# Eight operand splits issued later and in program order, one small vector operation moved in the last product, and 64-byte gaps between the weight tiles of a two-layer decoder trunk

## The chip, the cores and the metric

The kernel runs on one core of a Trainium2 chip. The metric is the time of one execution on the device in microseconds (us). Three runs of the kernel before took 1043.71, 1044.87 and 1045.28 us; their median is 1044.87 us.

A core has a matrix engine (PE; its weight loads are listed apart as PEld), a vector engine (DVE), an activation engine (ACT), a general engine (POOL) and a queue engine (SP) that issues most transfers. Each of them works through its own list of instructions in order and waits at the head of its list for what the next instruction needs.

## What is computed

The reference is two layers on 1024 tokens of width 1024. The first is a gated layer over chunks of 128 tokens, the second is attention with a window of 128 tokens, 16 query heads and 4 key and value heads, one sink per head and a linear bias. Each layer ends in a product with an output matrix, a root-mean-square norm and a residual sum. What the change touches lies in the second layer:

```python
q, z = jnp.split(h @ w_in, 2, axis=-1)
...
logits = jnp.einsum('btkgd,bskd->bkgts', qb, kb).astype(jnp.float32) + alibi
...
p = jnp.exp(logits - m[..., None])
denom = jnp.sum(p, axis=-1) + jnp.exp(sink - m)
o = jnp.einsum('bkgts,bskd->btkgd', p.astype(vb.dtype), vb).astype(jnp.float32)
...
y = out * jax.nn.silu(z)
return y @ w_out
```

## The kernel before, in words

Operands are float32. Each operand of a large product is kept as a high part and a low part: `split` (L104 to L106) lets ACT copy the source to `hi` (L105) and DVE write `lo`, the source less `hi` (L106). `mm3` (L215 to L218) makes a product from three matmuls: hi by hi, hi by lo, lo by hi. Such a matmul is 128x128 by 128x512. The large products are done in the seven-product scheme for 2x2 blocks, so that some operands are sums of blocks.

The phases in order are the first layer (`v_layer`, `uz_layer`, `out_layer`), the products for queries, keys and values, and then `attn`. `attn` goes through 16 units, each one block of 128 tokens and one half of the heads. Beside the work of the units it hands out 120 pieces of other work, the fill: 80 steps of query and gate products, and then 40 steps `p0` to `p39` of the output product (`Out.early`). A step of the output product is six matmuls. The list `BY` (L1283) says up to which fill step each unit goes, and the string `ORDER` (L1281) says in which order a pass takes its parts: scores of both head groups, fill, exponentials, values of the unit two passes back, fill, exponentials, gate, normalise, transposes of the unit one pass back, post, fill, fill, normalise. Unit 15, the last, is worked on while steps `p19` to `p25` are handed out; its scores come ahead of `p19`, and the values of unit 13 right behind `p19`. The steps `p0` to `p15` write PSUM tiles `oc`, `p16` to `p23` write `od`, `p24` to `p39` write `oe`.

The products behind `p24` and behind `p32` need a sum of blocks as their operand, four token blocks t = 0 to 3 each; these are called sum m = 1 and sum m = 7. `Out.sums` (L1352) makes each of them in three moves at three steps that the table `SUMS` (L1284) gives as (m, t, load, add, split): at the first number `y_again` loads a block from DRAM into a tile of the tag `raw` (which has three buffers), at the second POOL adds the gated block to it (for m = 1 the sum goes into another tile), at the third `split` makes the operand's `hi` and `lo`. The move for step k is written behind the product's step k. The steps `p24` to `p27` read sum m = 1 for t = 0 to 3, and `p32` to `p35` read sum m = 7 for t = 0 to 3.

The order in the lists of the engines is the work of a scheduler, which may take an instruction early when its model says that the inputs are there. `held` (L1287) ties the attention parts on DVE and ACT to one another in the order written; fill instructions are free, unless `tc.keep_in_program_order` ties one behind the instruction that was written before it on the same engine.

`Out.late` is the end: the product `of`, 96 matmuls, first the half that `after3` closes and then, for each t, 12 matmuls, an add of the PSUM tile (`c`), its square sum on ACT, a product with the gain (`o`), and the norm's factor `r`, which POOL raises to the power -0.5. `final` (L1306) makes output rows, two DVE operations at L1309, for the t before. One DVE operation at L1447 turns the square sums of the first half into `ef` for all four t.

Tiles in the on-chip memory lie in pools one behind another: `big` (operands T, n, q, o), `const`, `wpool` (three `raw`, two `whi`, two `wlo` tiles of 4096 bytes per partition, in this order), `st`, and then pools that take turns. In the built program every tile of `big`, `wpool` and `st`, and all further ones that are matmul weights or the large moving operands, starts at 128 modulo 256 bytes. The identity used by the transposes (`ident`) starts at 96 modulo 256, and the tiles `pr` at 32.

Of the kernel before, what the change touches and what calls it, by code (L numbers as in the profile page):

```python
# [7 lines left out]
F32 = mybir.dt.float32  # L8
F32R = mybir.dt.float32r
BF16 = mybir.dt.bfloat16  # L10
U32 = mybir.dt.uint32
AF = mybir.ActivationFunctionType
ALU = mybir.AluOpType

P = 128
D = 1024
# [8 lines left out]
EPS = 1e-6  # L25
# [25 lines left out]
def tile_yoco(  # L51
# [19 lines left out]
    nc = tc.nc  # L71
# [4 lines left out]
    wpool = ctx.enter_context(tc.tile_pool(name="wpool", bufs=2))  # L76
# [4 lines left out]
    def bank(tag, name):  # L81
        return psum.tile([P, 512], F32, tag=tag, name=name)
# [8 lines left out]
    small = const.tile([P, 5], F32, name="small")  # L91
    nhalf = small[:, 0:4]
    nc.vector.memset(nhalf, -0.5)

    def raw_tile(name):
        return wpool.tile([P, 1024], F32, tag="raw", name=f"raw_{name}", bufs=3)
# [7 lines left out]
    def split(hi, lo, src):  # L104
        nc.scalar.activation(hi, src, AF.Copy)  # L105
        nc.vector.tensor_tensor(lo, src, hi.bitcast(F32), ALU.subtract)  # L106
# [19 lines left out]
    class Weights:  # L126
# [30 lines left out]
        def load(self, i):  # L157
            for n in range(min(len(self.raw), 20), min(i, 19) + 1):
                src, kind = self.order[n]
                if n < 20:  # L160
                    self.raw[n] = wload(src, f"w{n}")
# [48 lines left out]
    def wnext():  # L210
        w = weights.get()
        weights.ahead()
        return w

    def mm3(out, a_hi, a_lo, b_hi, b_lo, start, stop):  # L215
        nc.tensor.matmul(out, lhsT=a_hi, rhs=b_hi, start=start, stop=False, skip_group_check=True)  # L216
        nc.tensor.matmul(out, lhsT=a_hi, rhs=b_lo, start=False, stop=False, skip_group_check=True)  # L217
        nc.tensor.matmul(out, lhsT=a_lo, rhs=b_hi, start=False, stop=stop, skip_group_check=True)  # L218
# [33 lines left out]
    def add(out, a, b, op, eng=None):  # L252
        (eng or nc.vector).tensor_tensor(out, a, b, op)  # L253
# [297 lines left out]
    def uz_layer():  # L551
# [153 lines left out]
        for q in range(len(quads) + 1):  # L705
# [24 lines left out]
            if q > 0:  # L730
                product(q - 1, 3, pcc, False)
                add(pc[0, 1], pc[0, 1], pcc, ALU.add)
                scale(pc[0, 1], 1)
                if pz:
                    finish(pg, 0, 1)
                    sums(pg)
                    del grp[pg]
                else:
                    for i in range(2):
                        for j in range(2):  # L740
                            nc.scalar.activation(pc[i, j], pc[i, j], AF.Gelu_apprx_tanh)
                del ops[q - 1]
# [331 lines left out]
    def by_head(t):  # L1074

        return t.rearrange("p k t -> p (k t)").rearrange("p (m b g t) -> p m b g t", m=4, g=2, t=P)
# [204 lines left out]
    ORDER = "01FavFbgmtpFFn"  # L1281
    lags = {}
    BY = [6, 12, 19, 25, 32, 38, 45, 51, 57, 64, 71, 78, 85, 92, 99, 106, 112, 120]  # L1283
    SUMS = [(1, 0, 0, 2, 17), (1, 1, 3, 5, 18), (1, 2, 6, 8, 19), (7, 0, 8, 11, 18), (1, 3, 10, 12, 20), (7, 1, 14, 16, 21), (7, 2, 19, 21, 24), (7, 3, 23, 25, 28)]  # L1284
    behind = {}

    def held(what, *args):  # L1287
# [18 lines left out]
    def final(h, t, yo, r, xt, later=None):  # L1306
        for i in range(2):
            cs = slice(i * 512, i * 512 + 512)
            nc.vector.scalar_tensor_tensor(yo[i], yo[i], r, xt[:, cs], ALU.mult, ALU.add)  # L1309
            dst = out[h * TH + t * P:h * TH + (t + 1) * P, cs]  # L1310
            if later is not None:
                later.append((dst, yo[i]))
            else:
                (nc.scalar if (h, t, i) == (1, 3, 1) else nc.sync).dma_start(out=dst, in_=yo[i])
# [4 lines left out]
    def y_again(p, t):  # L1319
        r = raw_tile(f"y{p}_{t}_{len(again)}")  # L1320
        again[len(again)] = r
        load(r[:, 0:512], yd[p][t])
        return r[:, 0:512]

    class Out:
# [26 lines left out]
        def sums(self, plan):  # L1352
            todo = {}
            for m, t, *at in plan:
                for what in range(3):
                    todo.setdefault(at[what], []).append((what, m, t))
            raw = {}
            for at in range(max(todo) + 1):
                for what, m, t in todo.get(at, ()):
                    if what == 0:  # L1360
                        raw[m, t] = y_again(m == 1, t)
                    elif what == 1:
                        d = self.s1[t] if m == 1 else raw[m, t]
                        mix = [a.rearrange("p (a t) -> p a t", t=P) for a in (d, raw[m, t])]
                        add(mix[0], mix[1], self.z[0][:, :, t * P:(t + 1) * P], ALU.add, nc.gpsimd)
                        raw[m, t] = d
                    else:
                        if m not in self.o:
                            self.o[m] = big.tile([P, 2, 4, 4, P], F32R, tag={1: "P0a", 7: "P0b"}[m], name=f"o{m}")
                        split(*(self.o[m][:, e, t].rearrange("p m t -> p (m t)") for e in range(2)), raw[m, t])  # L1370
                yield

        def early(self):
# [31 lines left out]
            def products():  # L1405
                ps = [bank("mm", f"oc{t}") for t in range(4)]
                yield from self.product(ps, self.of(self.q0, 0), True, True, lambda t, p: copy(m4[t], p))
                yield from self.product(ps, self.of(self.q0, 1), False, True, after2)
                ps = [bank("mm", f"od{t}") for t in range(4)]
                yield from self.product(ps, self.of(self.q1, 0), True, True, after5)  # L1410
                ps = [bank("mm", f"oe{t}") for t in range(4)]
                yield from self.product(ps, sum_operand(1), True, True,
                                        lambda t, p: add(n2[t], n2[t], p, ALU.add))
                yield from self.product(ps, sum_operand(7), False, True, after7)

            sums = self.sums(SUMS)
            for _ in products():
                step(sums)
                yield

        def late(self):
            gp, n2, m5, q1 = self.gp, self.n2, self.m5, self.q1
            ps = [bank("s", f"of{t}") for t in range(4)]

            def after3(t, p):
                c = m5[t]
                add(c, c, p, ALU.add)
                self.square(1, 0, t, c)
                add(c, c, gp[0], ALU.mult, nc.gpsimd)

            for k, _ in enumerate(self.product(ps, self.of(q1, 1), True, False, after3)):
                if k < 4:
                    d = self.z[1][:, :, k * P:(k + 1) * P]
                    hi, lo = (by_head(w)[:, 0:2, k] for w in q1)
                    split(hi, lo, d.rearrange("p (m g) t -> p m g t", m=2))
                elif k == 4:
                    w = [wnext() for _ in range(2)]
                    for dst, src in self.stores:
                        tc.keep_in_program_order(nc.sync.dma_start(out=dst, in_=src))
                elif k == 5:  # L1440
                    final(*self.rest.pop(0))
                elif k == 6:
                    hf = big.tile([P, 4, D], F32, tag="P0a", name="hf1")
                    xt = [load(hf[:, t], h1d[1][t]) for t in range(4)]
            final(*self.rest.pop(0))
            ef = const.tile([P, 8], F32, tag="rpa", name="ef1")
            nc.vector.tensor_scalar(ef[:, 0:4], self.ss[1][:, 0], 1.0 / D, EPS, ALU.mult, ALU.add)  # L1447
            y = self.of(q1, 0)
            for t in range(4):
                for m in range(4):  # L1450
                    hi, lo = w[m // 2]
                    cs = slice(m % 2 * 512, m % 2 * 512 + 512)
                    a = y(t, m)
                    mm3(ps[t], a[0], a[1], hi[:, cs], lo[:, cs], False, m == 3)
                c, o, r = n2[t], self.m4[t], ef[:, 4 + t:5 + t]
                add(c, c, ps[t], ALU.add)
                self.square(1, 1, t, c)
                add(o, c, gp[1], ALU.mult)
                if t:
                    final(*self.rest.pop(0))  # L1460
                nc.vector.tensor_scalar(r, self.ss[1][:, 1, t:t + 1], 1.0 / D, ef[:, t:t + 1], ALU.mult, ALU.add)
                nc.gpsimd.tensor_tensor(r, r, nhalf[:, 0:1], ALU.pow)
                self.rest.append((1, t, [m5[t], o], r, xt[t]))
            final(*self.rest.pop(0))
# [85 lines left out]
```

## Time and profile before

| | |
|---|---|
| median of three runs | 1044.87 us |
| the profiled execution's own time | 1044.52 us |
| its span in the profile | 1042.8 us |
| mean granted PE clock | 0.993 |
| first matmul of step `p0` starts | 930.53 us |
| last matmul starts | 1033.10 us |

The profile is of one execution. Busy time is the time an engine spends in instructions; matmuls overlap, so that the start of the next one says more than the length of one. A row of the timeline has the start in us, the length in us, engine, line of the kernel, operation, the tile written and the tiles read, shapes, and the number of instructions merged into the row; in brackets stands how long the engine was idle just before it and what released it. A row of the windows view has, for each engine, the busy time and the number of instructions in a stretch of time, and then the granted clock of PE and the share of the transfer engines. L106 is line 106 of the kernel.

### The profile page before, as it was taken

What the parts mean: (1) busy time and instruction counts of PE and PEld (TensorE: products, weight loads), DVE (VectorE), ACT (ScalarE), POOL (GpSimd) and SP (SyncE); (2) the same over time, 40 slices, a digit from 0 to 9 for tenths busy, and PEclk for the clock granted to TensorE, in tenths of its full rate; (3) what the DMA queues carried; (4) which work ended last, traced back from release to release, by engine and by line L of the source; (5) the groups of instructions that cost most, each with busy time, mean ns of one, the idle gap of its engine ahead of it and who ended that gap; (6) DMA issues with size and microseconds to landing.
All of it is one profiled execution on the core that took longest, in us unless ns stands there. A gap on an engine that the chain in (4) does not pass through costs nothing.

```text
span 1042.8 us, 14527 instructions
## 1 busy us (share of the span) xinstructions
PE 1025.3 (98%) x5186; PEld 839.6 (81%) x5186; DVE 792.4 (76%) x1342; ACT 541.1 (52%) x1018; POOL 276.2 (26%) x257
## 2 busy tenths in 40 slices
PE   9999999999999999999999999999999999999896
PEld 7888788888888888888878888888987777777575
DVE  6987467899898998988697777655166658787778
ACT  6684444565665565755445465444145445556332
POOL 0000004384664755743200000000001113244244
PEclk9999999999999999999999999999999999999898
DMA  8877353445555455457998651996135544334465
GB/s 313 273 277 287 101 175 116 151 152 176 173 162 172 134 184 157 157 176 254 316 388 311 203 203 53 349 352 241 51 143 190 176 149 142 112 106 146 173 222 202
DMA packets 117672, 203.83 MB, mean 195 GB/s; under 512 B 7776, under 2 KB 59872, under 8 KB 117600
## 3 DMA queue, kind: packets, MB, share of 16 engines
q1 hardware_dynamic: 113088, 194.22, 54.4%
q10 hardware_dynamic: 4512, 8.68, 2.4%
q8 instruction: 41, 0.67, 0.3%
q14 instruction: 31, 0.25, 0.1%
HBM read 142.05 MB, written 60.82 MB: 195 GB/s over the span
## 4 chain that ended last, share of the span: by engine, by line
PE 74%; DVE 7%; DMA 7%; issue 5%; ACT 3%; POOL 2%; SPq 1%; POOLq 0%; DVEq 0%; ACTq 0%
PE qz L216 5%; PE ub L216 5%; PE ub L218 5%; PE ub L217 5%; PE qz L218 5%; PE qz L217 5%; PE sp L659 2%; PE uc L217 2%; PE uc L216 2%; PE uc L218 2%; PE o L1218 2%; PE s L1155 2%; PE ob L218 2%; PE ob L216 2%; PE ob L217 2%
## 5 line engine op out<-in xcount | busy, mean ns | idle before, releaser
L1175 ACT ACTIVATE pr<-pr,mx 128x129 f32<-128x129 f32 x128 | 50.2, 394 | 56.3 <-DVE mx L1169 56.2
L216 PE MATMUL qz<-n_hi,whi_w 128*128 128x512 f32 x192 | 77.3, 403 | 0.0
L218 PE MATMUL qz<-n_hi,wlo_w 128*128 128x512 f32 x192 | 75.1, 391 | 0.1
L217 PE MATMUL qz<-n_lo,whi_w 128*128 128x512 f32 x192 | 74.9, 390 | 0.0
L803 POOL TENSOR_TENSOR presum<-presum_raw 128x128 f32<-128x128 f32 x80 | 49.1, 645 | 91.9 <-DMA od<-presum 84.8
L110 DVE SCALAR_TENSOR_TENSOR wlo_w<-raw_w,gn,whi_w 128x512 fp32r<-128x512 f32 x40 | 28.7, 748 | 48.6 <-ACT whi_w L109 48.5
L109 ACT ACTIVATE whi_w<-raw_w,gn 128x512 fp32r<-128x512 f32 x40 | 27.1, 715 | 63.2 <-PE pv L218 30.4
L253 POOL TENSOR_TENSOR f<-raw_uz 128x512 f32<-128x512 f32 x15 | 20.3, 1356 | 124.4 <-DMA raw_uz<-in_wuz_in_dram 105.6
L1195 POOL TENSOR_SCALAR_AFFINE_SELECT pc<-pc 128x1024 f32<-128x1024 f32 x16 | 20.1, 1259 | 121.6 <-DVE wlo_w L110 108.8
L216 PE MATMUL ub<-T,uzhilo_g 128*128 128x512 f32 x128 | 50.7, 396 | 0.9 <-ACT uz_slots L256 0.9
L106 DVE TENSOR_TENSOR uzhilo_g<-f,uzhilo_g 128x1024 fp32r<-128x1024 f32 x31 | 47.3, 1526 | 5.4 <-ACT uzhilo_g L105 5.4
L216 PE MATMUL ub<-T,whi_g 128*128 128x512 f32 x128 | 50.8, 397 | 0.0
L812 DVE TENSOR_TENSOR presum<-presum 128x128 fp32r<-128x128 f32 x80 | 50.6, 681 | 0.1
L218 PE MATMUL ub<-T,wlo_g 128*128 128x512 f32 x128 | 50.0, 391 | 0.0
L218 PE MATMUL ub<-T,uzhilo_g 128*128 128x512 f32 x128 | 49.9, 390 | 0.0
L217 PE MATMUL ub<-T,uzhilo_g 128*128 128x512 f32 x128 | 49.9, 390 | 0.0
L217 PE MATMUL ub<-T,whi_g 128*128 128x512 f32 x128 | 49.9, 390 | 0.0
L105 ACT ACTIVATE uzhilo_g<-f 128x1024 fp32r<-128x1024 f32 x31 | 32.8, 1057 | 32.2 <-PE uc L218 25.9
L216 PE MATMUL uc<-T,uzhilo_g 128*128 128x512 f32 x124 | 49.0, 395 | 0.0
L256 ACT ACTIVATE uz_slots<-ub 128x512 f32<-128x512 f32 x48 | 28.2, 587 | 39.7 <-PE ub L218 37.4
L217 PE MATMUL uc<-T,uzhilo_g 128*128 128x512 f32 x124 | 48.3, 390 | 0.0
L218 PE MATMUL uc<-T,uzhilo_g 128*128 128x512 f32 x124 | 48.3, 390 | 0.0
(399 smaller groups left out, 3301.0 us busy)
## 6 DMA issues: line engine op xcount, KB each, us to landing
raw_uz<-in_wuz_in_dram SPq DMA_DIRECT2D x32, 512.0 KB, 3.7
td<-uz_slots SPq DMA_DIRECT2D x56, 256.0 KB, 2.2
orawP2a<-td SPq DMA_DIRECT2D x28, 512.0 KB, 4.3
od<-presum SPq DMA_DIRECT2D x16, 640.0 KB, 4.0
raw<-in_wv_in_dram SPq DMA_DIRECT2D x17, 512.0 KB, 5.5
vg<-vd SPq DMA_DIRECT2D x8, 1024.0 KB, 5.6
orawP2b<-in_wo_a_dram SPq DMA_DIRECT2D x16, 512.0 KB, 8.0
raw_w<-in_wqz_dram SPq DMA_DIRECT2D x16, 512.0 KB, 5.1
```

The costliest lines, as they stand in the source:

```text
L105: nc.scalar.activation(hi, src, AF.Copy)
L106: nc.vector.tensor_tensor(lo, src, hi.bitcast(F32), ALU.subtract)
L109: nc.scalar.activation(hi, src, AF.Copy, scale=g)
L110: nc.vector.scalar_tensor_tensor(lo, src, g, hi.bitcast(F32), ALU.mult, ALU.subtract)
L216: nc.tensor.matmul(out, lhsT=a_hi, rhs=b_hi, start=start, stop=False, skip_group_check=True)
L217: nc.tensor.matmul(out, lhsT=a_hi, rhs=b_lo, start=False, stop=False, skip_group_check=True)
L218: nc.tensor.matmul(out, lhsT=a_lo, rhs=b_hi, start=False, stop=stop, skip_group_check=True)
L256: nc.scalar.activation(out, a, AF.Copy)
L659: nc.tensor.matmul(psv[:, n], lhsT=d["vg"][:, 4 * j + n, i * P:(i + 1) * P], rhs=d["wc"], start=True, stop=True)
L803: tc.keep_in_program_order(nc.gpsimd.tensor_tensor(o, a, b, op))
L812: tc.keep_in_program_order(nc.vector.tensor_tensor(t[:, k], lo[k], hi.bitcast(F32), ALU.subtract))
L1175: nc.scalar.activation(pr[:, i], pr[:, i], AF.Exp, bias=mx[:, i:i + 1], scale=-1.0, accum_out=dn[:, i:i + 1])
```

## The change

There are four edits.

Gaps: three tiles of 64 bytes per partition (`gap0` to `gap2`) are put into `wpool` and written once by DVE with zeros, and tiles named `..._first` that nothing reads fix the order of the tags: three `raw`, gap, two `whi`, gap, two `wlo`, gap. The `raw` tiles stay at 128 modulo 256, `whi` comes to 192, `wlo` to 0, and all that lies behind `wpool` to 64 bytes less modulo 256 (from 128 to 64), `st` and the pools that take turns among it.

Table: in `SUMS` the split steps are 18, 20, 22, 25, 23, 27, 29, 31 in the place of 17, 18, 19, 18, 20, 21, 24, 28. The last row's load moves from step 23 to 26 and its add from 25 to 27.

Order: the `hi` and `lo` of these eight splits are tied behind what was written before them on ACT and on DVE.

End: in `Out.late` the operation of L1447 is written behind the two DVE operations of t = 0, no more ahead of the loop.

```diff
@@ const tiles @@
+    def gap(i):
+        nc.vector.memset(wpool.tile([P, 16], F32, tag=f"gap{i}", name=f"gap{i}", bufs=1), 0.0)
+
+    for tag, rows in (("raw", 3), (None, 0), ("whi", 2), (None, 1), ("wlo", 2), (None, 2)):
+        if tag is None:
+            gap(rows)
+        else:
+            for i in range(rows):
+                wpool.tile([P, 1024], F32 if tag == "raw" else F32R, tag=tag, name=f"{tag}_first{i}", bufs=rows)
@@ attn @@
-    SUMS = [(1, 0, 0, 2, 17), (1, 1, 3, 5, 18), (1, 2, 6, 8, 19), (7, 0, 8, 11, 18), (1, 3, 10, 12, 20), (7, 1, 14, 16, 21), (7, 2, 19, 21, 24), (7, 3, 23, 25, 28)]
+    SUMS = [(1, 0, 0, 2, 18), (1, 1, 3, 5, 20), (1, 2, 6, 8, 22), (7, 0, 8, 11, 25), (1, 3, 10, 12, 23), (7, 1, 14, 16, 27), (7, 2, 19, 21, 29), (7, 3, 26, 27, 31)]
@@ Out.sums @@
-                        split(*(self.o[m][:, e, t].rearrange("p m t -> p (m t)") for e in range(2)), raw[m, t])
+                        hi, lo = (self.o[m][:, e, t].rearrange("p m t -> p (m t)") for e in range(2))
+                        tc.keep_in_program_order(nc.scalar.activation(hi, raw[m, t], AF.Copy))
+                        tc.keep_in_program_order(
+                            nc.vector.tensor_tensor(lo, raw[m, t], hi.bitcast(F32), ALU.subtract))
@@ Out.late @@
             ef = const.tile([P, 8], F32, tag="rpa", name="ef1")
-            nc.vector.tensor_scalar(ef[:, 0:4], self.ss[1][:, 0], 1.0 / D, EPS, ALU.mult, ALU.add)
             y = self.of(q1, 0)
@@
                 add(o, c, gp[1], ALU.mult)
-                if t:
+                if t == 0:
+                    nc.vector.tensor_scalar(ef[:, 0:4], self.ss[1][:, 0], 1.0 / D, EPS, ALU.mult, ALU.add)
+                else:
                     final(*self.rest.pop(0))
```

## The prediction

> **What bounds the kernel now.** I read the page first, then the windows view over the last 80 us, then the timeline of each engine where PE has a hole, and the chain of waits for what it hangs on.
>
> ```profile
> span 1042.8 us, 14527 instructions
> PE 1025.3 (98%) x5186; PEld 839.6 (81%) x5186; DVE 792.4 (76%) x1342; ACT 541.1 (52%) x1018; POOL 276.2 (26%) x257
> ```
>
> PE is busy for 98% of the span, so the kernel gets shorter only where PE's work itself gets cheaper, where a hole in PE closes, or behind the last matmul. The windows view finds the one large hole:
>
> ```profile
> 966.00:969.20 3.20, 3.20 (x31) 2.46 (x30) 3.20 (x7) 0.26 (x1) 0.00 (x0) 1.00 0.13 33
> 969.20:972.20 3.00, 0.01 (x1) 0.00 (x1) 2.96 (x11) 0.00 (x0) 1.34 (x1) 1.00 0.46 125
> 972.20:977.10 4.90, 3.77 (x16) 1.11 (x16) 3.00 (x16) 2.28 (x9) 0.13 (x1) 0.73 0.95 342
> 977.10:981.90 4.80, 4.80 (x14) 3.75 (x13) 2.53 (x5) 2.73 (x10) 2.41 (x2) 0.56 0.45 174
> 981.90:988.30 6.40, 6.40 (x34) 5.37 (x33) 5.21 (x7) 3.29 (x6) 2.67 (x3) 1.00 0.28 93
> 988.30:1011.50 23.20, 23.20 (x125) 17.56 (x124) 15.33 (x24) 9.40 (x17) 6.52 (x6) 1.00 0.62 224
> ```
>
> From 969.2 to 972.2 PE does nothing while DVE is full (2.96 of 3.00 us). Then the granted clock falls to 0.73 and 0.56 and is back at 1.00 in the last two rows. The hole costs its own length and, behind it, a slow stretch. Next come PE's rows: an undisturbed pass of the same parts first (values of unit 12 behind `p12`), then the disturbed one (values of unit 13 behind `p19`).
>
> ```profile
> 954.96 0.40 PE L218 MATMUL oc<-wm_w,q_lo 128*128 128x512 f32 x1
> 955.29 0.65 PE L1218 MATMUL o<-pc,vt 64*64 64x512 f32 x2
> ...
> 956.74 0.50 PE L216 MATMUL oc<-wm_w,q_hi 128*128 128x512 f32 x1
> ...
> 967.34 0.28 PE L1155 MATMUL s<-k,q_hi 64*128 64x192 f32 x2
> ...
> 968.81 0.40 PE L218 MATMUL od<-whi_w,q_lo 128*128 128x512 f32 x1
> 972.23 1.08 PE L1218 MATMUL o<-pc,vt 64*64 64x512 f32 x4 [3.02 <-DVE mx L1169]
> 974.41 1.93 PE L1218 MATMUL o<-pp,vt 64*64 64x512 f32 x8 [1.11 <-DVE mx L1169]
> ...
> 977.12 0.79 PE L216 MATMUL od<-whi_w,q_hi 128*128 128x512 f32 x1
> ...
> 981.92 1.04 PE L1189 MATMUL pt<-ident,pr 128*128 128x128 f32 x8
> ...
> 988.26 1.03 PE L1189 MATMUL pt<-ident,pr 128*128 128x128 f32 x8
> ...
> 1011.56 0.39 PE L216 MATMUL of<-whi_w,q_hi 128*128 128x512 f32 x1
> ...
> 1033.10 0.39 PE L218 MATMUL of<-whi_w,q_lo 128*128 128x512 f32 x1
> ```
>
> The last two rows are the first and the last of 96 matmuls without a break: (1033.10 - 1011.56)/95 = 0.227 us from one start to the next. That is PE's step at full clock. The values of unit 13 wait for DVE at L1169: they need the PSUM banks that the scores of unit 15 fill, and DVE has to read those out. DVE's rows say why it is late:
>
> ```profile
> 953.13 0.30 DVE L1162 COPY_PREDICATED s<-mrg,s 128x128 f32<-128x128 uint32 x1 [2.67 <-PE s L1155]
> ...
> 963.49 1.57 DVE L106 TENSOR_TENSOR q_lo<-z,q_hi 128x512 fp32r<-128x512 f32 x1
> ...
> 966.18 1.28 DVE L106 TENSOR_TENSOR o<-sum_P2b,o 128x512 fp32r<-128x512 f32 x2
> ...
> 969.93 1.28 DVE L106 TENSOR_TENSOR o<-raw_yFalse,o 128x512 fp32r<-128x512 f32 x2
> 971.13 0.28 DVE L1162 COPY_PREDICATED s<-mrg,s 128x128 f32<-128x128 uint32 x1
> ...
> 973.03 0.69 DVE L106 TENSOR_TENSOR o<-raw_yFalse,o 128x512 fp32r<-128x512 f32 x1 [0.74 <-ACT o L105]
> ```
>
> The score matmuls end at about 967.6 and DVE turns to them at 971.13, because low parts of the sums stand ahead of them. The groups by line between 960 and 990 count eight:
>
> ```profile
> L106 DVE TENSOR_TENSOR o<-raw_yFalse,o 128x512 fp32r<-128x512 f32 x4 | 2.7, 682 | 0.7 <-ACT o L105 0.7
> L106 DVE TENSOR_TENSOR o<-sum_P2b,o 128x512 fp32r<-128x512 f32 x4 | 2.6, 672 | 0.0
> ```
>
> Seven lie between 966.18 and 971.13. None is read before `p24`, two steps behind the transposes at 981.92. The eighth, at 973.03, cuts in between the two banks; its way there:
>
> ```profile
> 963.09 1.43 POOL L1195 TENSOR_SCALAR_AFFINE_SELECT pc<-pc 128x1024 f32<-128x1024 f32 x1
> ...
> 968.09 0.32 SPq L270 DMA_DIRECT2D raw_yFalse<-yd  x1
> 970.86 1.47 POOL L253 TENSOR_TENSOR raw_yFalse<-raw_yFalse,z 128x512 f32<-128x512 f32 x1 [6.34 <-DMA raw_yFalse<-yd]
> 972.37 0.63 ACT L105 ACTIVATE o<-raw_yFalse 128x512 fp32r<-128x512 f32 x1 [6.11 <-POOL raw_yFalse L253]
> ```
>
> Its load had to wait for a free `raw` buffer, POOL added behind it, and ACT held the exponentials of unit 15 behind its high part until 973.0.
>
> **The change part by part: table and order.** With the new steps only (m = 1, t = 0), at step 18, stays ahead of the scores of unit 15. Six of the seven low parts leave the place ahead of 971.13, at some 0.62 us each (two start to end in 1.28, overlapping by a little): 3.7 us. DVE could then begin on the scores at 967.4. In the undisturbed pass the values start 955.29 - 953.13 = 2.2 us behind DVE's begin, so here at 969.6, where `p19` ends at 968.81 + 0.23 = 969.04. A hole of 0.5 us stays.
>
> What the hole costs now: from 969.04 to 977.12 are 8.08 us, and the undisturbed pass needs 956.74 - 955.19 = 1.55, so 6.5 us go to waits and to the clock. The twelve matmuls of `p20` and `p21` take 981.92 - 977.12 = 4.80 us where 12 x 0.227 = 2.73, so 2.1 more. Together 8.6 us. Without them the transposes of unit 15, now at 988.26, could be issued at 979.7.
>
> The splits have to go somewhere, and DVE is what is late next. The transposes of unit 15 need its normalise, behind `p25`. DVE's busy time from 966.0 to 988.3 sums to 3.20 + 2.96 + 3.00 + 2.53 + 5.21 = 16.9 us. Two adds of 0.6 each at its end come behind the normalise, and three low parts (m = 7, t = 1 to 3) now go behind it at 0.68 each: 13.6 us stay, so without any idle DVE is through at 979.6. It will have some: it waits for ACT's copy of the values and for the exponentials. I take 1.2 us, so the transposes start at 980.8 and the gain is 7.5 us. Behind them DVE has room (15.33 us busy of 23.20 in the last window), and three more low parts cost nothing.
>
> The ties add waits. The splits at steps 20, 22, 23 stand behind ACT's copies of finished `od` tiles, and behind them stand exponentials of unit 15 on ACT and its normalise on DVE. From the step of the split to the step that reads it are 4 to 7 steps of 6 x 0.227 = 1.36 us, against about 1.3 us for `hi` and `lo`. The load of (7, 3) moves to step 26 and waits for the buffer that the split at step 25 frees. On SP the loads of output weights for `of` stand behind it (read only at 1011.56), so that waiting costs nothing; from step 26 to its reader `p35` are nine steps, 12 us, and load, add and split take 968.09 to 973.72, under 6 us.
>
> **End.** Two rows of DVE and one of POOL:
>
> ```profile
> 1024.47 3.21 POOL L253 TENSOR_TENSOR sum_P2b<-sum_P2b,gpb 128x512 f32<-128x512 f32 x2 [0.34 <-ACT junk_b L1350]
> ...
> 1026.45 1.25 DVE L1447 TENSOR_SCALAR ef<-ssb 128x4 f32<-128x4 f32 x1
> 1027.62 0.67 DVE L253 TENSOR_TENSOR sum_P2a<-sum_P2a,of 128x512 f32<-128x512 f32 x1
> ...
> 1034.82 0.68 DVE L253 TENSOR_TENSOR sum_P2a<-sum_P2a,of 128x512 f32<-128x512 f32 x1
> ```
>
> The small operation at L1447 takes 1.25 us and ends when POOL ends (1027.68). The last add begins at 1034.82, 1.5 us behind the last matmul's slot, so DVE leads there. With L1447 behind the adds, the first add starts at 1026.45, 1.17 us earlier; that is the upper bound. The next operation, `o`, has both inputs in on-chip memory, as the one at 963.49 that took 1.57 us in the place of 0.68 while POOL was busy from 963.09 on, and may wait for POOL till 1027.68 too. Then it ends at 1028.35, where it now ends two operations behind 1027.62, at 1029.0. I take 0.6 us, the lower bound 0.
>
> The Trainium skill, SBUF — State Buffer, section Who interferes with whom, says that a DVE instruction with two inputs in SBUF is blocked while a POOL instruction that reads SBUF holds the port, and the reverse. The trace agrees (1.57 against 0.68 us); by that rule the moved low parts, which are of this kind, also can cost 0.9 us more each where POOL's work meets them.
>
> **Gaps.** The three writes are of the kind of this row and lie in DVE's idle time before its first real work:
>
> ```profile
> 1.01 0.06 DVE L93 MEMSET small<- 128x4 f32 x1
> ...
> 4.46 0.69 DVE L461 TENSOR_TENSOR wlo_v<-raw_v,whi_v 128x512 fp32r<-128x512 f32 x1 [3.38 <-POOL whi_v L458]
> ```
>
> At about 0.1 us each they are hidden by 3.38 us of idle time. For the other placement the trace of before has no row: weights and large operands all start at 128 modulo 256. The nearest are 128-column matmuls:
>
> ```profile
> L659 PE MATMUL sp<-wc,vg 128*128 128x128 f32 x256 | 31.1, 275 | 0.0
> L1189 PE MATMUL pt<-ident,pr 128*128 128x128 f32 x128 | 16.6, 272 | 0.0
> ```
>
> The first has both operands at 128, the second has them at different places; 3 ns apart, and they differ in more than the place. Over 5186 matmuls 3 ns are 15.6 us. That bounds the gaps at 15.6 us either way. I take nothing: a product and a transpose may differ by 3 ns without any help of the place.
>
> The Trainium skill, TensorE: Matmul & The Clock Gate, section What happens when you issue a matmul, says that the moving operand and the weight load have read ports of their own, so that loading weights takes nothing from a running matmul; by it the gaps are worth nothing. No run here shows it yet.
>
> **Sum.** 7.5 + 0.6 = 8.1 us. The profiled execution took 1044.52 us, 1.7 more than its span and 0.35 less than the median; it would become 1036.4, and the median 1044.87 - 8.1 = 1036.8.
>
> **The rivals.** First, the hole moves (0.14): DVE, now short of idle time, is late for the transposes of unit 15. The 2.53 us of 4.80 and 3.00 of 4.90 that DVE is busy in the middle windows speak against it, the blocked operations for it. Five low parts at 1.57 - 0.68 = 0.9 us more each are 4.5 us; if that turns into a hole of 3 us with a slow stretch of 2.1 us, 3 us of the gain stay: 1041.9, and down to no gain.
>
> Second, slower (0.11): the new placement makes weight load and moving operand meet. It decides from 8.1 us/5186 = 1.6 ns per matmul on; at the 3 ns bound the kernel takes 1036.8 + 15.6 = 1052.4. For it speaks that with the present places 96 matmuls in a row keep 0.227 us without a break, so that a change has more to spoil than to mend; against it that of the two rows the one with unequal places is the shorter.
>
> Third, the same the other way (0.06), for which that shorter row speaks: 1036.8 - 15.6 = 1021.2.
>
> Fourth, the change does nothing (0.04), if the scheduler still puts the low parts first: 1044.9. The ties speak against it, as they stand behind copies that need `od`.
>
> **How the numbers follow.** The forecast has 0.65: from 1044.87 - 8.6 - 1.2 = 1035.1 to 1039.5. A measurement can tell 0.2%, or 2.1 us, from no change. Faster: 0.65 + 0.06 + 0.09 of the first rival = 0.80. Same: 0.05 of the first and 0.04 of the fourth = 0.09. Slower: 0.11. The range leaves out the second and third rivals and takes in most of the first: 1034.5 to 1043.5.
>
> **What would show it.** Right: no PE row with a wait for L1169 above 1 us behind `p19`, granted clock 1.00 from 966 to the end of `of`, DVE at the scores of unit 15 within 1 us of PE, transposes of unit 15 near 981, low parts of the sums spread over `p18` to `p31`, a PE step of 0.227 us as before. Wrong: a hole ahead of the transposes of unit 15 or of `p24` to `p27` or `p32` to `p35`, or another PE step in stages where `whi` or `wlo` is read but not in those where both operands lie in `big` (`ob<-ohiloP0b,ohiloP0a`).

## The result, and the profile after

The changed kernel takes 1051.22 us (median of four runs, 1050.34 to 1052.09), the kernel before 1045.07 us beside it. The ratio is 1.0048, with a 95% interval of 1.0031 to 1.0065; the two medians alone give 1.0059, which lies inside it. The change makes the kernel slower, by about half a per cent; the prediction had 1036.8 us and a range up to 1043.5.

The head of the page of the changed kernel:

```profile
span 1049.2 us, 14536 instructions
PE 1035.6 (99%) x5186; PEld 839.0 (80%) x5186; DVE 795.2 (76%) x1345; ACT 541.5 (52%) x1018; POOL 275.8 (26%) x257
```

PE makes the same 5186 matmuls and is busy 10.3 us longer (1025.3 before). The span grew by 6.4 us, so PE has fewer holes and slower work. The windows of the changed kernel, over the stages that the prediction looked at:

```profile
977.22:980.40 3.18, 3.18 (x33) 2.54 (x34) 3.08 (x14) 0.60 (x3) 0.00 (x0) 1.00 0.04 15
980.40:985.00 4.60, 4.60 (x29) 3.13 (x30) 3.62 (x15) 3.86 (x16) 0.56 (x1) 1.00 0.73 224
985.00:993.60 8.60, 7.30 (x37) 5.80 (x35) 8.45 (x13) 5.17 (x12) 5.30 (x4) 1.00 0.36 127
993.60:1016.60 23.00, 23.00 (x122) 17.12 (x123) 14.34 (x20) 8.79 (x15) 6.37 (x5) 1.00 0.60 207
1016.60:1039.30 22.70, 22.56 (x97) 17.78 (x95) 22.03 (x37) 7.46 (x22) 15.88 (x14) 1.00 0.77 275
```

The granted clock is 1.00 in every row, and PE is without work for 1.3 us in the third and 0.1 us in the last. The large hole is closed. PE's timeline in the changed kernel, with the landmarks that the prediction used:

```profile
941.31 0.39 PE L226 MATMUL oc<-wm_w,q_hi 128*128 128x512 f32 x1
...
993.60 1.07 PE L1199 MATMUL pt<-ident,pr 128*128 128x128 f32 x8 [1.29 <-DVE pr L1192]
...
1016.59 0.39 PE L226 MATMUL of<-whi_w,q_hi 128*128 128x512 f32 x1
...
1039.07 0.40 PE L228 MATMUL of<-whi_w,q_lo 128*128 128x512 f32 x1
```

Step `p0` starts at 941.31 us in the place of 930.53. So 10.8 us are lost before any of the moved splits has been issued (a table further down shows how far this point scatters). From there to the transposes of unit 15 half of that is won back: they start 5.3 us later than before (993.60 against 988.26), `of` 5.0 and the last matmul 6.0 us later. Two effects of opposite sign are added up here.

The loss shows in the views by tile. Their columns are line, engine, operation, tile written and tiles read, count, then the least, median and largest duration of one matmul in ns. The kernel before:

```profile
L216 PE MATMUL vb<-whi,T x72: 388/389/398, 39.5 to 149.9; 128*128 128x512 f32 x72
L217 PE MATMUL vb<-wlo,T x72: 388/389/390, 39.7 to 150.1; 128*128 128x512 f32 x72
...
L216 PE MATMUL ob<-ohiloP0b,ohiloP0a x48: 388/389/390, 498.7 to 602.4; 128*128 128x512 f32 x48
L216 PE MATMUL ob<-whi_s,ohiloP0a x40: 388/389/390, 504.1 to 607.8; 128*128 128x512 f32 x40
```

The changed kernel:

```profile
L226 PE MATMUL vb<-whi,T x72: 388/397/397, 40.8 to 152.9; 128*128 128x512 f32 x72
L227 PE MATMUL vb<-wlo,T x72: 387/387/396, 41.1 to 153.2; 128*128 128x512 f32 x72
...
L226 PE MATMUL ob<-ohiloP0b,ohiloP0a x48: 389/389/393, 505.6 to 610.1; 128*128 128x512 f32 x48
L226 PE MATMUL ob<-whi_s,ohiloP0a x40: 397/397/398, 511.0 to 615.6; 128*128 128x512 f32 x40
```

Before, the median of each of these groups is 389 ns. After, the two groups that read the moved `whi` have 397 ns and the one that reads the moved `wlo` 387, while `ob<-ohiloP0b,ohiloP0a`, with both operands in `big`, keeps 389. In most other groups that read a moved tile the median is 390 to 398 ns. This is the sign that the prediction named for its second rival. From the starts of the 512-column matmuls, leaving out steps of 260 ns or more (breaks), the mean step went from 227.4 ns (some 3750 steps) to 231.0 ns (some 3760). That is 3.54 ns x 3760 = 13.3 us of PE time.

### The profile page after: what moved, and what is told of

Its sections match the earlier page's. It is cut to its first block, busy times and chain, and to the rows that moved or that the text cites. A ratio compares the mean times of both kernels' runs of the same rounds, so it can differ in the third digit from the quotient of the medians.

```text
span 1049.2 us, 14536 instructions
## 1 busy us (share of the span) xinstructions
PE 1035.6 (99%) x5186; PEld 839.0 (80%) x5186; DVE 795.2 (76%) x1345; ACT 541.5 (52%) x1018; POOL 275.8 (26%) x257
## 4 chain that ended last, share of the span: by engine, by line
PE 88%; DVE 5%; DMA 3%; ACT 2%; issue 1%; POOL 1%; SPq 0%; POOLq 0%; DVEq 0%; ACTq 0%
PE qz L226 5%; PE ub L226 5%; PE ub L228 5%; PE ub L227 5%; PE qz L228 5%; PE qz L227 5%; PE oc L226 3%; PE ob L226 3%; PE ob L228 3%; PE ob L227 3%; PE oc L228 3%; PE oc L227 3%; PE sp L669 3%; PE vb L228 3%; PE vb L227 3%; PE uc L228 3%
## 5 line engine op out<-in xcount | busy, mean ns | idle before, releaser
L226 PE MATMUL qz<-n_hi,whi_w 128*128 128x512 f32 x192 | 78.6, 409 | 0.3 <-ACT whi_w L119 0.3
L228 PE MATMUL qz<-n_hi,wlo_w 128*128 128x512 f32 x192 | 75.6, 394 | 0.1
L226 PE MATMUL ub<-T,whi_g 128*128 128x512 f32 x128 | 51.6, 403 | 0.0
L226 PE MATMUL ub<-T,uzhilo_g 128*128 128x512 f32 x128 | 50.6, 396 | 0.4 <-ACT uz_slots L266 0.3
L228 PE MATMUL ub<-T,uzhilo_g 128*128 128x512 f32 x128 | 50.4, 394 | 0.0
L228 PE MATMUL ub<-T,wlo_g 128*128 128x512 f32 x128 | 50.2, 392 | 0.0
L226 PE MATMUL uc<-T,uzhilo_g 128*128 128x512 f32 x124 | 49.0, 395 | 0.0
L228 PE MATMUL uc<-T,uzhilo_g 128*128 128x512 f32 x124 | 48.9, 394 | 0.0
```

## The experiments

The theory at this point: the gaps cost some 10 us, because a matmul is slower when the weights being loaded lie at another place modulo 256 bytes than the operand being streamed; the new order gives some 4 to 6 us. Its rivals: the gaps cost through something else (the address itself, the early claim of the tiles, the writes), or the new order is what costs and the gaps add little.

**The new order alone, the gaps alone, the table alone.** The first kernel is the change without its first hunk, the second the kernel before with that hunk only, the third the kernel before with the new `SUMS` and nothing else:

```diff
@@ order alone: the change without @@
-    for tag, rows in (("raw", 3), (None, 0), ("whi", 2), (None, 1), ("wlo", 2), (None, 2)):
...
@@ gaps alone: before, with @@
+    for tag, rows in (("raw", 3), (None, 0), ("whi", 2), (None, 1), ("wlo", 2), (None, 2)):
...
@@ table alone: before, with @@
+    SUMS = [(1, 0, 0, 2, 18), (1, 1, 3, 5, 20), (1, 2, 6, 8, 22), (7, 0, 8, 11, 25), (1, 3, 10, 12, 23), (7, 1, 14, 16, 27), (7, 2, 19, 21, 29), (7, 3, 26, 27, 31)]
```

Expected of the order alone: 

> The change without the gaps: table, ties and the moved operation alone. Theory P (place): the step from one 128x512 matmul to the next grows from 0.227 us to 0.229 to 0.236 us where the weights being loaded and the operand being streamed start at different bytes modulo 256; the gaps cost about 13 us and the other three edits save about 7. Then this kernel takes 1037 to 1039 us and its steps are 0.227 us as before. Rival S (schedule): the longer steps come with the other order of the work, and this kernel takes about 1051 us, with steps of 0.229 to 0.236 us.

Expected of the gaps alone: 

> The kernel before with the gaps alone. Theory P: about 1045 + 13 = 1058 us, steps as in the changed kernel, the hole of 3 us behind p19 and the slow clock behind it still there. Rival S: 1045 us and steps of 0.227 us.

Expected of the table alone: 

> The kernel before with the new table of steps alone, splits not tied, end as before. If the later steps are what takes the low parts out of the way of the scores of unit 15: 1038 to 1039 us. If the ties are needed, since the scheduler takes free splits early in any case: 1044 to 1045 us and the wait for L1169 stays.

| kernel | median us | before, same chip | ratio (95%) |
|---|---|---|---|
| order, without gaps | 1041.90 | 1046.10 | 0.9959 (0.9947 to 0.9972) |
| gaps alone | 1056.06 | 1046.10 | 1.0098 (1.0070 to 1.0125) |
| table alone | 1044.66 | 1046.10 | 0.9985 (0.9971 to 0.9998) |

The two parts add up: -4.2 and +10.0 make +5.8 us, and the whole change measured +6.15. The theory had 1037 to 1039 us for the order alone and about 1058 for the gaps alone: the order brings less than it said, the gaps cost somewhat less. PE's waits behind 960 us say what the order did. The table alone, and then the order without gaps:

```profile
PE o L1218 <- DVE mx L1169: 3.0, 1, 3.0
```

```profile
PE pt L1189 <- DVE pr L1182: 1.4, 1, 1.4
PE of L216 <- DMA whi_w<-od: 0.8, 1, 0.8
```

With the table alone the long wait for L1169 is as before (3.0 us): the scheduler still takes the low parts early, and it needs the ties to move them. What the table alone gains, 1.4 us on the median, goes with a second wait for L1169 of 1.1 us that is no longer there. With the ties the long wait is gone, and two small ones come in its place; the second was not in the prediction.

**Which places cost.** A kernel of matmuls and nothing else (the computation is left out) runs 24 matmuls of 128x128 by 128x512 for each pair of places:

```diff
+    for m, w in CASES:
+        ps = psum.tile([P, 512], F32, tag=f"b{j % 4}", name=f"m{m}w{w}x")
+        run(ps, m, w, N)
```

Expected: 

> Leaves out the whole computation of the reference and does nothing but matmuls 128x128 by 128x512, 24 for each of 43 pairs of places: moving operand at 128, 0, 64 and 192 modulo 256 bytes, weights at 0 to 224 bytes behind it in steps of 32, and finer steps at 128. No other engine works beside them. Theory P: 0.227 us a step where both are at the same place, whatever that place is, and 0.229 to 0.236 us elsewhere. Rival S, and a rival by which it takes other engines' traffic to make the places matter: the same step for all pairs. If some pair is below 0.227 us, another placement would make the kernel faster.

In its timeline `m128w192x` is the moving operand at 128 and the weights at 192 modulo 256. The next row's start less a row's own, over 24, is the step:

```profile
21.29 5.62 PE L94 MATMUL m128w128x<-mov,wei 128*128 128x512 f32 x24
26.74 5.75 PE L94 MATMUL m128w160x<-mov,wei 128*128 128x512 f32 x24
32.33 5.76 PE L94 MATMUL m128w192x<-mov,wei 128*128 128x512 f32 x24
37.93 5.77 PE L94 MATMUL m128w224x<-mov,wei 128*128 128x512 f32 x24
...
54.74 5.67 PE L94 MATMUL m128w64x<-mov,wei 128*128 128x512 f32 x24
60.25 5.76 PE L94 MATMUL m128w96x<-mov,wei 128*128 128x512 f32 x24
65.85 5.61 PE L94 MATMUL m0w0x<-mov,wei 128*128 128x512 f32 x24
71.30 5.75 PE L94 MATMUL m0w32x<-mov,wei 128*128 128x512 f32 x24
```

Equal places: (26.74 - 21.29)/24 = 0.227 us, and the same at 0 (65.85 to 71.30). With the weights 32 bytes further the step is 0.233 us (26.74 to 32.33), 64 further 0.233 (32.33 to 37.93), 192 further 0.230 (54.74 to 60.25). With the moving operand at 128, 0, 64 or 192 the same distance gives the same step within 0.3 ns, but for the equal pair at 64, whose first steps are longer (228.5 ns in the mean, 227.3 from the ninth on). Of the finer distances, weights 4 and 16 bytes short of the operand are as good (226.7 ns once settled), but 8 bytes short is not (233.3), nor are 4, 8 and 16 bytes beyond it (231.0 to 233.3). No distance was faster than an equal place by more than 0.2 ns. So nothing was to be won in this sweep, and most distances cost 6 to 7 ns.

**Not the address itself.** Here the kernel before gets one 64-byte tile ahead of `big`, so that every tile moves by the same 64 bytes:

```diff
+    ahead = ctx.enter_context(tc.tile_pool(name="ahead", bufs=1))
     big = ctx.enter_context(tc.tile_pool(name="big", bufs=1))
...
+    nc.vector.memset(ahead.tile([P, 16], F32, name="ahead64"), 0.0)
```

Expected: 

> The kernel before with one 64-byte tile ahead of all the others, so that every tile, weights and operands alike, begins 64 bytes later and weights and operands keep the same place modulo 256; the step order and the operation at the end are those of before. Theory A (only the place of the weights against the moving operand counts): no change, 1045 us within 2 us, matmul step 227 ns. Rival B (the place itself counts, 128 being the good one): every 512-column step is 229 to 234 ns as in the run with the gaps alone, 1053 to 1060 us.

Measured: 1046.38 us against 1046.11, ratio 1.0007 (0.9986 to 1.0029). Its row:

```profile
L218 PE MATMUL vb<-whi,T x72: 387/389/390, 40.7 to 150.7; 128*128 128x512 f32 x72
```

389 ns as before, at 192 in the place of 128.

**Not the claim of the tiles.** The whole change, with one gap of 256 bytes in the place of three of 64:

```diff
-        nc.vector.memset(wpool.tile([P, 16], F32, tag=f"gap{i}", name=f"gap{i}", bufs=1), 0.0)
+        nc.vector.memset(wpool.tile([P, 64], F32, tag=f"gap{i}", name=f"gap{i}", bufs=1), 0.0)
-    for tag, rows in (("raw", 3), (None, 0), ("whi", 2), (None, 1), ("wlo", 2), (None, 2)):
+    for tag, rows in (("raw", 3), (None, 0), ("whi", 2), ("wlo", 2)):
```

Expected: 

> The whole change, but with one gap of 256 bytes (between the raw and the high weight tiles) in place of three of 64, so that the tiles are claimed in the same order and with gap memory, and weights and operands stand at the same place modulo 256 again. Theory A (the loss is the unequal place modulo 256 alone): the time of the change without gaps, 1041.9 us within 1 us, matmul step 227.4 ns. Rival B (another address order, the early claim of the tiles or the memsets cost): 1045 to 1051 us.

Measured: 1041.48 us against 1046.07, ratio 0.9951 (0.9937 to 0.9964): the time of the order without gaps. Its row:

```profile
L226 PE MATMUL vb<-whi,T x72: 388/389/395, 40.2 to 151.5; 128*128 128x512 f32 x72
```

Between this kernel and the change lie only the size and number of the gaps. With the kernel in which all tiles move, this shows the cause of the loss: unequal places modulo 256.

**Why unequal places cost.** Matmuls alone again (the computation is left out), with 128, 64 and 32 weight columns and 512, 384 and 256 moving columns:

```diff
+CASES = [(d, c, n) for n in (512, 384, 256) for c in (128, 64, 32) for d in (0, 64, 128)]
```

Expected: 

> Runs of 24 matmuls and nothing else (the computation is left out): weights of 128, 64 and 32 columns, moving operands of 512, 384 and 256 columns, weights 0, 64 or 128 bytes from the place of the moving operand modulo 256. Theory A (the extra 6 to 7 ns of unequal places arises while the next weights are read beside the moving operand): the extra is the same in ns at 512, 384 and 256 columns, and shrinks with fewer weight columns, to under 4 ns at 64 and under 2 at 32. Rival B (the moving operand's own reads are slower at another place): the extra shrinks with the moving columns, to half at 256, and is the same for all weight widths. Rival C (a fixed cost per switch of weights): the same extra in all nine.

Measured, step in ns (mean of the last 20 steps of each run) for weights 0, 64 and 128 bytes from the moving operand:

| moving columns | 128 weight columns | 64 | 32 |
|---|---|---|---|
| 512 | 226.7, 233.3, 231.9 | 229.8, 232.7, 229.3 | 231.7, 231.7, 230.7 |
| 384 | 174.4, 176.7, 176.0 | 173.3, 173.3, 173.3 | 173.3, 174.6, 173.2 |
| 256 | 119.7, 117.8, 118.7 | 113.3, 113.3, 116.7 | 113.3, 113.3, 113.3 |

Three of its rows, with 128 columns of weights and 256 of the moving operand:

```profile
109.41 3.03 PE L93 MATMUL d0c128n256x<-mov,wei 128*128 128x256 f32 x24
112.27 2.99 PE L93 MATMUL d64c128n256x<-mov,wei 128*128 128x256 f32 x24
115.10 3.01 PE L93 MATMUL d128c128n256x<-mov,wei 128*128 128x256 f32 x24
```

None of the three theories fits. At 64 bytes the extra is 6.6 ns at 512 columns and 128 weight columns and 2.3 ns at 384 columns (3.4 from the ninth matmul on, when the equal place has settled at 173.3), and at 256 the equal place is the slower one (2.86/24 = 0.119 us from row to row, then 2.83/24 = 0.118). At 512 columns the extra shrinks with narrower weights because the step at equal places grows, from 226.7 to 231.7 ns. So the good step of 227 ns belongs to full weights and 512 columns at equal places; what in the reads makes it so stays open.

**The small operation at the end.** The order without gaps, with L1447 at its old place:

```diff
+            nc.vector.tensor_scalar(ef[:, 0:4], self.ss[1][:, 0], 1.0 / D, EPS, ALU.mult, ALU.add)
...
-                if t == 0:
-                    nc.vector.tensor_scalar(ef[:, 0:4], self.ss[1][:, 0], 1.0 / D, EPS, ALU.mult, ALU.add)
-                else:
+                if t:
```

Expected: 

> The new table and the two tied halves, without the gaps, and with the small operation of the end left at its old place (L1447). Theory A (moving it brings nothing, since the chain of final operations behind it leads): 1041.9 us as with the move, within 0.6 us, and 6.6 to 7.0 us from the last matmul to the last VectorE operation. Rival B (the move costs, because the final operations grew from 6.64 to 7.02 us): 1041.4 us. Rival C (it brings the 0.6 us of the prediction): 1042.5 us.

Measured: 1041.68 us, ratio 0.9965 (0.9945 to 0.9985), where the move had 0.9959. The times can't tell the three theories apart. From the last matmul to the last DVE operation this kernel takes 8.2 us, where theory A had 6.6 to 7.0; a comparison further down settles the matter.

**Vector halves with steps of their own.** The order without gaps; each low part gets its own step, those of (7,0) to (7,2) go behind the normalise of unit 15, and one fill step goes ahead of the transposes in the last passes:

```diff
-    SUMS = [(1, 0, 0, 2, 18), (1, 1, 3, 5, 20), (1, 2, 6, 8, 22), (7, 0, 8, 11, 25), (1, 3, 10, 12, 23), (7, 1, 14, 16, 27), (7, 2, 19, 21, 29), (7, 3, 26, 27, 31)]
+    SUMS = [(1, 0, 0, 2, 18, 18), (1, 1, 3, 5, 20, 20), (1, 2, 6, 8, 22, 22), (7, 0, 8, 11, 25, 26), (1, 3, 10, 12, 23, 23), (7, 1, 14, 16, 25, 26), (7, 2, 19, 21, 25, 26), (7, 3, 26, 28, 31, 31)]
-            for what in ORDER if i < len(units) else "tvgpFFFF":
+            for what in ORDER if i < len(units) else "FtvgpFFF":
```

Expected: 

> The change without the gaps, and the VectorE halves of the splits get steps of their own: those of (7,0), (7,1) and (7,2) come one step behind their ScalarE halves, placed behind the normalise of unit 15, and the steps of the last two turns begin with one fill step ahead of the transposes. So the raw buffers come free earlier than in the change without gaps. Theory A (the late raw loads cost about 1 us in front of the third weight pair of the stage called of): the loads start before 985, the 1.0 us hole in front of it closes and the time is 1040.5 to 1041.3 us against 1041.9. Rival B (the fill step that now stands ahead of the transposes only moves the wait, and the transposes come later by as much): 1041.9 to 1043.

Measured: 1040.15 us against 1046.11, ratio 0.9947 (0.9929 to 0.9966), a little under theory A. SP's timeline in the order without gaps, and then in this kernel:

```profile
996.45 1.57 SPq L101 DMA_DIRECT2D raw_w<-in_wo_b_dram  x2
...
1013.44 0.38 SPq L150 DMA_DIRECT2D whi_w<-od  x1
```

```profile
984.63 0.97 SPq L101 DMA_DIRECT2D raw_w<-in_wo_b_dram  x2
...
1011.30 0.38 SPq L150 DMA_DIRECT2D whi_w<-od  x1
```

In the first the two loads of output weights wait for `raw` buffers that the late splits free, and are issued at 996.45 us. The first load of `raw_hf`, behind them on SP, is pushed back too (from 973.75 to 999.49). From 1008 to 1020 the transfer engines are then full (DMA share 1.01), and `whi_w` takes 7.6 us from issue to landing, where it takes 5.4 us before and in the second kernel. That is the 0.8 us wait in front of the weights of `of`. In the second kernel it is gone (DMA share 0.73 from 1010 to 1017), and the wait ahead of the transposes, which the moved fill step shortens, is 0.2 us:

```profile
PE pt L1189 <- DVE pr L1182: 0.2, 1, 0.2
```

**The same kernel once more, and with the old end.** These ran beside the kernel with one gap of 256 bytes. The old-end kernel has the hunk of the small operation above.

Expected of the kernel again: 

> The kernel with the separate steps for the VectorE halves again, beside the change without any offset (the run with one gap of 256 bytes) on the same chip. Theory A (the late raw loads cost about 1 us and the residual wait ahead of the transposes another 1): 1.3 to 2.2 us below that run. Rival B (they differ only by chips and chance): within 0.6 us of it.

Expected of the one with the old end: 

> As the kernel with the separate steps for the VectorE halves (measured 1040.15 us), with the small operation of the end at its old place. If the move brings nothing, the two agree within 0.5 us; if it costs, this one is 0.4 us faster, if it brings what the prediction said, 0.6 us slower.

Measured: 1039.71 us, ratio 0.9944 (0.9927 to 0.9961), and 1038.97 us, ratio 0.9930 (0.9918 to 0.9943), where the kernel with one gap of 256 bytes had 1041.48. The vector halves with steps of their own gain 1.8 us on the median over the plain order, though the intervals overlap; with the old end they make the fastest kernel of the study. Of the two ends the medians favour the old one by 0.7 us. The vector engine's timeline, the old end first:

```profile
1018.38 1.78 DVE L1309 SCALAR_TENSOR_TENSOR sum_P2a<-sum_P2a,ef,hf 128x512 f32<-128x512 f32 x1
1020.09 1.25 DVE L1452 TENSOR_SCALAR ef<-ssb 128x4 f32<-128x4 f32 x1
1021.25 0.67 DVE L253 TENSOR_TENSOR sum_P2a<-sum_P2a,of 128x512 f32<-128x512 f32 x1
...
1022.91 0.68 DVE L253 TENSOR_TENSOR sum_P2a<-sum_P2a,of 128x512 f32<-128x512 f32 x1
```

```profile
1019.10 1.78 DVE L1309 SCALAR_TENSOR_TENSOR sum_P2a<-sum_P2a,ef,hf 128x512 f32<-128x512 f32 x1
1020.81 0.67 DVE L253 TENSOR_TENSOR sum_P2a<-sum_P2a,of 128x512 f32<-128x512 f32 x1
1021.51 1.08 DVE L253 TENSOR_TENSOR sum_P<-sum_P2a,gpb 128x512 f32<-128x512 f32 x1
1022.51 0.16 DVE L1464 TENSOR_SCALAR ef<-ssb 128x4 f32<-128x4 f32 x1
...
1022.91 0.68 DVE L253 TENSOR_TENSOR sum_P2a<-sum_P2a,of 128x512 f32<-128x512 f32 x1
```

From the last `final` before the adds to the second add the old end takes 4.53 us, the moved one 3.81. The move saves 0.72 us there, but this profiled execution was 0.72 us later at that point, as at the start of `p0` (930.71 against 929.99) and at its last matmul (1025.60 against 1024.88). Times that scatter by 2 us and more cannot show such a step.

The stretch behind `p0` can. All moved work lies behind the first matmul of `p0`. The start of `p0` scatters by 3 us (929.99 to 932.99) between profiled executions of kernels that differ in nothing ahead of it:

| kernel | `p0` starts, us | span, us | from `p0` to the end, us |
|---|---|---|---|
| before | 930.53 | 1042.8 | 112.3 |
| before, all tiles moved by 64 bytes | 931.94 | 1044.4 | 112.5 |
| order, without gaps | 932.99 | 1040.6 | 107.6 |
| order, one gap of 256 bytes | 934.15 | 1041.7 | 107.6 |
| order, old end | 930.89 | 1039.1 | 108.2 |
| vector halves | 932.12 | 1037.9 | 105.8 |
| vector halves, again | 930.71 | 1036.4 | 105.7 |
| vector halves, old end | 929.99 | 1036.4 | 106.4 |

Pairs that should agree do so within 0.2 us. By this measure the order with the move gains 4.7 us, the vector halves 1.8 us more, and the move itself saves 0.6 and 0.7 us in its two pairs. So of the three expectations for the old end the last is right, by traces of one execution each. That the medians favour the old end by 0.7 us is put down to the scatter ahead of `p0`; this is argued, not shown.

## Why the prediction was wrong, point by point

**The step that failed** is the value of the gaps: "I take nothing". They cost 10.0 us. The change would have been faster without them (1041.90 us). The mechanism was the second rival, its price 2.6 ns when spread over all 5186 matmuls (13.3 us), near the 3 ns bound and above the 1.6 ns from which it decides. On the long matmuls alone it is 3.5 ns, above the bound. Of the 13.3 us of PE time 10.0 arrive in the median. Part of the difference lies behind `p0`: that stretch takes 107.9 us in the change, 0.3 more than without gaps, and the wait of 0.8 us for `whi_w` does not appear in it. That the second rival's 1052.4 us lies so near the measured 1051.2 is partly luck: it took the gaps 5.6 us too dear and the order 3.9 us too good.

The rows that the choice went by could not carry it. They compared 128-column matmuls, `sp` against `pt`; the width sweep shows that the effect is 6.6 ns at 512 columns, 2.3 at 384 and turned round at 256. `sp`, whose `wc` lies behind `wpool` and so moved to 64 while `vg` stayed at 128, has 275 ns before and after. The argument that 96 matmuls in a row at 227 ns have more to spoil than to mend was the better one: the bounds were not equally likely, since the sweep has no distance with a step much below that of equal places. The third rival, a gain of the same size, rested on the row of `pt` alone.

By the rule of the Trainium skill, TensorE: Matmul & The Clock Gate, section What happens when you issue a matmul, the weight load takes no read bandwidth from the running matmul. The runs differ: 226.7 or 233.3 ns, by the distance of the weights alone. That the two share something in the read is argued, not shown.

**The hole** went as predicted. The wait for L1169 is gone, the granted clock is 1.00 to the end of `of`, and DVE turns to the scores of unit 15 at 978.70 us, right behind the last of them:

```profile
978.70 0.29 DVE L1172 COPY_PREDICATED s<-mrg,s 128x128 f32<-128x128 uint32 x1
...
985.18 1.11 DVE L1383 TENSOR_TENSOR o<-sum_P2b,o 128x512 fp32r<-128x512 f32 x1
...
986.87 1.13 DVE L1192 TENSOR_TENSOR pr<-pr,dn 128x512 f32<-128x512 f32 x1
987.92 1.57 DVE L116 TENSOR_TENSOR q_lo<-z,q_hi 128x512 fp32r<-128x512 f32 x1
...
990.01 0.97 DVE L1383 TENSOR_TENSOR o<-sum_P2b,o 128x512 fp32r<-128x512 f32 x1
```

**The term of 7.5 us** came to 6.4 at the transposes of unit 15. From the scores of unit 15 to its transposes the kernel before needs 22.2 us (966.04 to 988.26), the order without gaps 16.5 us (968.50 to 985.00). That is 5.7 us, and 0.7 more are three matmuls of `p26` that now come ahead of the transposes. The prediction reckoned with 13.6 us of DVE work in this stretch and 1.2 us of idle time. The idle time was right (1.2 us), the work is 15.3 us. Two adds of `od` blocks, taken out of the sum because they come behind the second normalise in the kernel before, come ahead of it in the new order: 1.1 us. The five low parts take 3.7 us where the sum had 2.8 left for them, `q_lo` 1.5 where it had 1.2, and the normalises are 0.7 us shorter. The low parts stretch beside POOL. Its rows in the changed kernel:

```profile
984.44 1.30 POOL L263 TENSOR_TENSOR z<-z,z 128x512 f32<-128x512 f32 x1 [8.88 <-DVE z L1241]
985.82 1.63 POOL L263 TENSOR_TENSOR z<-sum_P2b,z 128x512 f32<-128x512 f32 x1
987.40 1.55 POOL L1204 TENSOR_SCALAR_AFFINE_SELECT pp<-pc 128x1024 f32<-128x1024 f32 x1
989.02 1.43 POOL L1205 TENSOR_SCALAR_AFFINE_SELECT pc<-pc 128x1024 f32<-128x1024 f32 x1
```

They end at 985.74, 987.45, 988.95 and 990.45 us. The four DVE operations above at 985.18, 986.87, 987.92 and 990.01, all with two inputs in on-chip memory, each end 0.5 to 0.6 us behind one of these ends. PE's wait for the second normalise, 1.29 us, is what is left of the hole: the first rival has its place right and its size wrong, since no slow stretch follows. These rows agree with the rule of the Trainium skill, SBUF — State Buffer, section Who interferes with whom, that the prediction told and used for its first rival, but not in this term.

**That the moved load costs nothing** was wrong. The late splits hold the `raw` buffers, the output weights and the first `raw_hf` load behind them come 26 us later than before (996.45 against 970.6 us), and the transfers crowd in front of `of`: a wait of 0.8 us, and a break of 1.0 us beyond the usual step. In the kernel with separate vector halves, which issues the two loads 12 us earlier, the wait is gone.

**The end** is worth its 0.6 us: 0.72 by the two timelines, 0.6 and 0.7 by the stretch behind `p0`. The prediction saw that DVE leads at the last add, and yet let the whole gain of PE reach the end. In `of` DVE is busy for 22.03 of 22.70 us in the change. From the last matmul to the last DVE operation the kernel before takes 6.6 us, the order with the same old end 8.2: 1.6 us of what PE gained ahead do not get past DVE there.

Together the order and the move of the small operation brought 4.2 us where 8.1 were forecast. By the profile of the order without gaps it is 6.4 for the hole, less 1.3 from the first to the last matmul of `of` (22.9 us in the place of 21.5), less 0.4 behind it (10.1 in the place of 9.7): 4.7, as from `p0` to the end. With the old end it is 112.3 - 108.2 = 4.1, so about 4 us of the term of 7.5 arrive.

## What to carry to other kernels

For matmuls of 128x128 by 128x512 like these, weights and the operand streamed beside them should start at the same place modulo 256 bytes; a small tile put between pools moves all that lies behind it, and the price is seen as a few ns on every matmul, in the view by tile, not as a wait. A cost that is bounded only by rows of another shape is not bounded: before it is set to nothing, ask which side of the bound has a state to lose. When splits are moved later, look at the buffers that they free and the loads that stand behind these in the queue. Where the early part of a kernel scatters from run to run, measure a late change from a landmark just ahead of it.

## What the runs showed of the hardware that was not expected

- The step of a 128x128 by 128x512 matmul is 226.7 ns with weights and moving operand at the same place modulo 256 bytes and 229 to 234 ns at the other distances tried in steps of 32 bytes. Moving both by 64 bytes changes nothing (389 ns durations, ratio 1.0007).
- Narrower weights do not bring the good step back: with 32 weight columns the step at 512 moving columns is 230.7 to 231.7 ns at each distance tried, the equal place included.
- In the kernel the price does not follow from the distance alone. In the sweeps, weights 64 bytes from the moving operand cost 6.6 ns, and 128 bytes 6.6 or 5.2. In the changed kernel the three matmuls of `qz` (L226 to L228, `n` beside `whi_w` and `wlo_w`) have weights 64, 64 and 128 bytes from the moving operand, and their mean steps are 235.7, 228.8 and 229.9 ns (227.8, 227.7 and 228.2 before). `vb<-wlo,T`, with 128 bytes between its operands, even has 225.0 ns in the place of 226.8, while its two neighbours in the same product lose 8.5 and 6.8. What else sets the price was not tried.
